# Row variance over 64 MB: increments of a semaphore at the end of two engines' programs, and a wait for them ahead of the clear

## The chip, the cores and the metric

The kernel runs on one core of one Trainium2 chip. The metric is the device time of one execution in microseconds (us). Three runs of the kernel before took 163.08, 163.54 and 163.08 us, a median of 163.08 us. The profiled execution took 163.1 us, and its span, from the first to the last of the program's own instructions, is 161.4 us.

## The reference: the variance of each row

The input is 32 x 512 rows of 1024 floats, 64 MB in all. For every row the kernel computes the mean of the squares less the square of the mean:

```python
mean_sq = np.mean(x**2, axis=-1)
sq_mean = np.mean(x, axis=-1)**2
return (mean_sq - sq_mean).astype(np.float32)
```

16,384 results are written, 64 KB.

## The kernel before

The 16,384 rows are laid on 128 partitions, 128 rows on each; the code calls one such row of every partition a column. `xt[0]` and `xt[1]` hold 16 columns each (8 MB a buffer). SyncE (SP in the profile) issues every load and every store, in the order in which they are written. Three turns of two buffers cover 96 columns; the last 32 columns come in pieces that grow smaller, `END_LOADS = [8, 8, 5, 4, 2, 2, 1, 1]`, and the very last column in two halves of 512 elements.

VectorE (DVE) and ScalarE (ACT) share the columns of each buffer. DVE takes a column with two BN_STATS of 512 elements and one BN_AGGR. ACT takes a column with two passes, `act_mean` (Copy with an accumulated sum, L122) and `act_var` (Square with the negative mean as bias and an accumulated sum, L127); the profile shows each of them as an ACTIVATE and an ACTIVATION_READ_ACCUMULATOR. In the loops ACT does 6 of 16 columns and DVE 10. In the last 32 columns the string `END_WHO` says who takes which; ACT has the column of the last full load, DVE the two halves after it. GpSimd (POOL) copies finished results and finishes 14 columns of the end from DVE's statistics.

Two details matter for the change. Both engines' programs are placed by `addr_align`, once, ahead of their loops (L145 and L146); in the profile that is a COMPARE_BRANCH of L146 on each of the two engines. The only code placed so is the engines' program from there on; nothing says where it ends.

The end of SP's program is a chain of waits and stores. The first store goes out after POOL's first copy (L304), the second when POOL, ACT and DVE have finished the columns before the last few (L306 to L309), and the third, 7 columns, when ACT has made its last step (L310, `act_step`) and DVE its last (L311, `dve_step`). SP then clears all semaphores but one (L313), waits for the three stores to land (L314) and clears the semaphore that they count (L315). The semaphores to clear are a range, from the first to the last in the list `sems` (L92).

DVE's program ends with the BN_AGGR of the last column (L262), which increments `dve_step`. ACT's program ends with the last `act_var` (L298), which increments `act_step`. After the program's own instructions the runtime's run: all engines meet, each resets a share of the semaphores, and they meet again.

Of the kernel before, what the change touches and what calls it, by code (L numbers as in the profile page):

```python
# [11 lines left out]
def kernel(  # L12
# [14 lines left out]
    nc = tc.nc  # L27
# [27 lines left out]
    PIECES = [512, 512]  # L55
    EARLY = 4
    HEAD = 128

    def sbuf(name, shape, dtype):
        return nc.alloc_sbuf_tensor(name, shape, dtype).ap()  # L60
# [19 lines left out]
    sync, act, dve, gps = nc.sync, nc.scalar, nc.vector, nc.gpsimd  # L80
    landed = [nc.alloc_semaphore(f"landed{b}") for b in range(NBUF)]
    NEND = len(END_LOADS) + len(PIECES)
    landed_end = [nc.alloc_semaphore(f"landed_end{b}") for b in range(NEND)]
    go = nc.alloc_semaphore("go")
    dve_done = nc.alloc_semaphore("dve_done")
    done = nc.alloc_semaphore("done")
    copied = nc.alloc_semaphore("copied")
    dve_step = nc.alloc_semaphore("dve_step")
    act_step = nc.alloc_semaphore("act_step")
    gps_step = nc.alloc_semaphore("gps_step")  # L90
    stored = nc.alloc_semaphore("stored")
    sems = [*landed, *landed_end, go, dve_done, done, copied, dve_step, act_step, gps_step]  # L92

    def load(dst, c0, n, sem, f0=0, f=D):
        b0, pitch, row0 = next(b for b in BLOCKS if b[0] <= c0 < b[0] + b[1])
# [7 lines left out]
    def store(c0, c1):  # L103
        b0, pitch, row0 = next(b for b in BLOCKS if b[0] <= c0 < b[0] + b[1])
        sync.dma_start(
            out=dataclasses.replace(
                out, offset=row0 + c0 - b0, ap=[[pitch, P], [1, c1 - c0]]
            ),
            in_=mv[:, 1, c0:c1],
        ).then_inc(stored, 16)  # L110
# [34 lines left out]
    for engine in (act, dve):  # L145
        engine.addr_align(FETCH_BLOCK_INSTRUCTIONS, offset=HEAD, max_nops=0)  # L146

# [113 lines left out]
    dve.wait_ge(dve_step, n)  # L261
    dve.bn_aggr(out=mv[:, :, c], in_=st).then_inc(dve_step, 1)  # L262
    dve_steps = n + 1

    act.preload_act_table(ACTF.Square)  # L265
    with nc.Fori(0, TURNS, engines=[ENG.Activation]):
# [18 lines left out]
    for b in range(len(END_LOADS)):  # L285
# [14 lines left out]
        last.then_inc(act_step, 1)  # L300
        act_step_of[b] = n
    act_steps = n

    sync.wait_ge(copied, 1)  # L304
    store(0, SMALL)
# [4 lines left out]
    sync.wait_ge(act_step, act_steps)  # L310
    sync.wait_ge(dve_step, dve_steps)  # L311
    store(early, ncols)
    sync.sem_clear(range(sems[0].num, sems[-1].num + 1))  # L313
    sync.wait_ge(stored, 48)  # L314
    sync.sem_clear(stored)  # L315
# [30 lines left out]
```

## Time and profile before

| | |
|---|---|
| median of three runs | 163.08 us |
| profiled execution, its own time | 163.1 us |
| its span | 161.4 us |
| DVE busy, ACT busy, POOL busy | 102.7, 106.9, 4.0 us |
| bytes read from HBM | 67.11 MB |
| load queue q1, share of 16 DMA engines' span | 97.1% |
| instruction queue q14 | 2 packets, 0.02 MB |

The times of single events below are microseconds from the span's start. A row of a group has the line in the kernel, the engine, the operation, what it writes from what it reads, the number of instructions, their busy time and the mean of one. SPq, ACTq and DVEq are the engines' sequencers: instructions that do no work on data, such as waits, increments and branches, are listed under these. Increments and waits that stand alone are EVENT_SEMAPHORE instructions, and clears of a range are EVENT_SEMAPHORE_RANGE_CLEAR. Besides instructions, the trace records each change of a semaphore and each packet of a DMA queue with its time; some times below are from these records.

### The profile page before, as it was taken

The numbers are of one execution on the slowest core, as the hardware profiler recorded it, in microseconds if no ns is written. First come the engines' busy times: TensorE is split into PE (matmuls) and PEld (weight loads), VectorE is DVE, ScalarE is ACT, GpSimd is POOL, SyncE is SP. The second block draws the span as 40 slices with busy tenths as digits, with TensorE's granted clock in tenths as the row PEclk, the third lists the DMA queues.
The fourth block names the chain that finished last, engine by engine and source line by source line (L and its number), as shares of the span: only waits on it lengthen the run. The fifth ranks groups of instructions, "written<-read, shape, count | busy, mean of one in ns | idle before, by whom it ended". The sixth has DMA issues, their size and how long they took to land. (4 is left out here: it accounts for less than half of the span.)

```text
span 161.4 us, 568 instructions
## 1 busy us (share of the span) xinstructions
DVE 102.7 (64%) x229; ACT 106.9 (66%) x189; POOL 4.0 (2%) x19
## 2 busy tenths in 40 slices
DVE  0000029980599607994099921999139999999894
ACT  3000039972599807996089941999339979999995
POOL 0000000000000000000000000000000000000700
DMA  7959969969969969969979979979969999899992
GB/s 264 520 260 520 520 276 503 520 276 503 520 276 503 520 276 504 520 292 487 520 309 471 520 325 455 520 325 455 520 276 471 422 406 479 380 424 416 426 396 77
DMA packets 2738, 67.19 MB, mean 416 GB/s; under 512 B 688, under 2 KB 688, under 8 KB 1200
## 3 DMA queue, kind: packets, MB, share of 16 engines
q1 hardware_dynamic: 2736, 67.18, 97.1%
q14 instruction: 2, 0.02, 0.1%
HBM read 67.11 MB, written 0.07 MB: 416 GB/s over the span
## 5 line engine op out<-in xcount | busy, mean ns | idle before, releaser
L118 DVE BATCH_NORM_STATS2 stats<-xt 128x6 f32<-128x512 f32 x120 | 71.8, 679 | 54.9 <-DVEq L114 54.9
L122 ACT ACTIVATE junk<-xt 128x1024 bf16<-128x1024 f32 x41 | 42.7, 1043 | 44.1 <-ACTq L114 43.7
L127 ACT ACTIVATE junk_sq<-xt,neg_mean 128x1024 f32<-128x1024 f32 x36 | 39.9, 1107 | 5.6 <-ACTq L114 4.1
L118 DVE BATCH_NORM_STATS2 stats_join<-xt 128x6 f32<-128x512 f32 x22 | 13.1, 681 | 0.0
L122 ACT ACTIVATION_READ_ACCUMULATOR junk<-xt 128x1 f32 x41 | 7.7, 187 | 0.0
L127 ACT ACTIVATE junk_sq<-xt_end,neg_mean_end 128x1024 f32<-128x1024 f32 x6 | 6.7, 1111 | 0.1
L127 ACT ACTIVATION_READ_ACCUMULATOR junk_sq<-xt,neg_mean 128x1 f32 x36 | 6.7, 187 | 0.0
L122 ACT ACTIVATE junk<-xt_end 128x1024 bf16<-128x1024 f32 x6 | 6.3, 1045 | 0.4 <-DMA xt_end<-in_x_dram 0.3
L220 DVE BATCH_NORM_AGGREGATE stage<-stats 128x2 f32<-128x12 f32 x60 | 5.1, 162 | 0.9
L127 ACT ACTIVATE junk_sq<-xt,neg_mean_end 128x1024 f32<-128x1024 f32 x5 | 5.5, 1105 | 0.1
L239 DVE BATCH_NORM_STATS2 stats_end<-xt_end 128x6 f32<-128x512 f32 x6 | 4.1, 683 | 0.6 <-DMA xt_end<-in_x_dram 0.6
L173 POOL COPY mv<-stage 128x32 f32<-128x32 f32 x3 | 0.6, 211 | 133.3 <-ACT junk_sq L127 133.3
L243 DVE BATCH_NORM_STATS2 stats_end<-xt_end 128x6 f32<-128x512 f32 x6 | 3.9, 646 | 0.0
L118 DVE BATCH_NORM_STATS2 stats_join<-xt_end 128x6 f32<-128x512 f32 x6 | 3.7, 692 | 0.0
L265 ACT ACT_TABLE_LOAD x1 | 1.3, 1283 | 2.8 <-PEq L153 2.8
L255 DVE BATCH_NORM_STATS2 stats_end<-xt_end 128x6 f32<-128x512 f32 x2 | 1.3, 668 | 0.6 <-DMA xt_end<-in_x_dram 0.6
L248 DVE BATCH_NORM_AGGREGATE mv<-stats_end 128x2 f32<-128x12 f32 x6 | 1.2, 194 | 0.0
L127 ACT ACTIVATION_READ_ACCUMULATOR junk_sq<-xt_end,neg_mean_end 128x1 f32 x6 | 1.1, 186 | 0.0
L122 ACT ACTIVATION_READ_ACCUMULATOR junk<-xt_end 128x1 f32 x6 | 1.1, 186 | 0.0
L127 ACT ACTIVATION_READ_ACCUMULATOR junk_sq<-xt,neg_mean_end 128x1 f32 x5 | 0.9, 186 | 0.0
L200 POOL TENSOR_SCALAR mv<-mu 128x6 f32<-128x6 f32 (+2 forms) x3 | 0.7, 238 | 0.3
L181 POOL TENSOR_TENSOR two<-stats_join 128x28 f32<-128x28 f32 x1 | 0.3, 273 | 15.0 <-DVE stats_join L118 15.0
(13 smaller groups left out, 2.8 us busy)
## 6 DMA issues: line engine op xcount, KB each, us to landing
xt<-in_x_dram SPq DMA_DIRECT2D x2, 4096.0 KB, 19.1
xt_end<-in_x_dram SPq DMA_DIRECT2D x1, 2560.0 KB, 29.4
xt_end<-in_x_dram SPq DMA_DIRECT2D x1, 2048.0 KB, 33.8
xt_end<-in_x_dram SPq DMA_DIRECT2D x2, 1024.0 KB, 36.8
xt_end<-in_x_dram SPq DMA_DIRECT2D x2, 512.0 KB, 38.9
xt_end<-in_x_dram SPq DMA_DIRECT2D x2, 256.0 KB, 39.6
xt<-in_x_dram SPq DMA_DIRECT2D x6, 24.1
out_dram<-mv SPq DMA_DIRECT2D x1, 52.5 KB, 4.4
```

The costliest lines, as they stand in the source:

```text
L118: last = dve.bn_stats(out=st[:, h, :], in_=xcol[:, h * H : (h + 1) * H])
L122: return act.activation(out=junk[i], in_=xcol, func=ACTF.Copy, scale=-S / D, accum_out=nm)
L127: return act.activation(out=junk_sq[i], in_=xcol, func=ACTF.Square, scale=S, bias=nm, accum_out=var)
L173: gps.tensor_copy(out=mv[:, 1, t * PER_TURN : (t + 1) * PER_TURN], in_=stage[:, :, 1]).then_inc(copied, 1)
L181: lambda: gps.tensor_tensor(out=two, in0=mean[:, :, 0:2], in1=mean[:, :, 2:4], op=ALU.add),
L200: lambda j=j, c=c, n=n: gps.tensor_scalar(out=mv[:, 1, c : c + n], in0=mu[:, j : j + n, 0], scalar1=1.0 / D, scalar2=None, op0=ALU.mult,)
L220: last = dve.bn_aggr(out=stage[:, j, :], in_=stats[:, j, :, :])
L239: dve.bn_stats(out=st[:, 0, :], in_=col[:, :H])
L243: dve.bn_stats(out=st[:, 1, :], in_=col[:, H:]).then_inc(dve_step, 1)
L248: return dve.bn_aggr(out=mv[:, :, c], in_=st)
L255: last = dve.bn_stats(out=st[:, i, :], in_=end_col(c)[:, f : f + size])
L265: act.preload_act_table(ACTF.Square)
```

## The change

A new semaphore `ended` is allocated and put into the list of those that SP clears. DVE increments it 8 times after its last BN_AGGR, ACT 16 times after its last `act_var`. These 24 increments are instructions of their own. SP waits until `ended` has reached 24 before its clear of the range. The wait stands behind the issue of the last store. Nothing else differs; the lines of the file move down by 3 to 8.

```diff
+    DVE_END = 8
+    ACT_END = 16
...
+    ended = nc.alloc_semaphore("ended")
     stored = nc.alloc_semaphore("stored")
-    sems = [*landed, *landed_end, go, dve_done, done, copied, dve_step, act_step, gps_step]
+    sems = [*landed, *landed_end, go, dve_done, done, copied, dve_step, act_step, gps_step, ended]
...
     dve.bn_aggr(out=mv[:, :, c], in_=st).then_inc(dve_step, 1)
     dve_steps = n + 1
+    for _ in range(DVE_END):
+        dve.sem_inc(ended, 1)
...
     act_steps = n
+    for _ in range(ACT_END):
+        act.sem_inc(ended, 1)
...
     store(early, ncols)
+    sync.wait_ge(ended, DVE_END + ACT_END)
     sync.sem_clear(range(sems[0].num, sems[-1].num + 1))
     sync.wait_ge(stored, 48)
     sync.sem_clear(stored)
```

## The prediction

> **What bounds the kernel now.** I read the page's head and its queues first, then the chain of waits that ended last, then the timeline of the last five microseconds, then SP's own waits. Page:
>
> ```profile
> span 161.4 us, 568 instructions
> ...
> DVE 102.7 (64%) x229; ACT 106.9 (66%) x189; POOL 4.0 (2%) x19
> ...
> q1 hardware_dynamic: 2736, 67.18, 97.1%
> q14 instruction: 2, 0.02, 0.1%
> ```
>
> The loads hold the 16 DMA engines for 97.1% of the span, and both compute engines are idle a third of it. The kernel is bound by its loads until they end. The second queue is the instructions': two packets in the whole span. The chain says the same, and what follows the loads:
>
> ```profile
> 118.15 39.35 DMA xt_end<-in_x_dram
> 157.50 0.02 issue
> 157.52 1.16 ACT junk L122 x2
> 158.68 0.02 issue
> 158.70 1.24 ACT junk_sq L127 x2
> ```
>
> The last full column lands at 157.50, and ACT's two passes over it, 1.16 and 1.24 us, end at 159.94. The change touches only what stands behind that. The timeline of the end:
>
> ```profile
> 158.91 0.64 DVE L255 BATCH_NORM_STATS2 stats_end<-xt_end 128x6 f32<-128x512 f32 x1
> 159.59 0.21 DVE L262 BATCH_NORM_AGGREGATE mv<-stats_end 128x2 f32<-128x12 f32 x1
> 159.75 0.19 ACT L127 ACTIVATION_READ_ACCUMULATOR junk_sq<-xt_end,neg_mean_end 128x1 f32 x1
> 159.97 0.33 SPq L105 DMA_DIRECT2D out_dram<-mv  x1
> ```
>
> The reader is to see that DVE ends at 159.80 and ACT at 159.94, that the last store is issued from 159.97 to 160.30, and that nothing computes after that. What is left of the span, 1.1 us, is SP's, and its waits name the one that ends last:
>
> ```profile
> SPq L311 <- DVE mv L262: 4.7, 1, 4.7
> SPq L315 <- DMA out_dram<-mv: 1.0, 1, 1.0
> ```
>
> By the records of single instructions the range clear (L313) runs from 160.343 to 160.407, and then SP sits until the store has landed at 161.361; the second clear runs from 161.378 to 161.403, the end of the span. So 0.97 us of SP's time after the first clear (161.378 less 160.407) is spent waiting for the store. That is the cover of the whole change.
>
> **The change part by part.**
>
> Sixteen increments on ACT. The nearest rows: in the loop a lone increment of `go` (L270) starts 72 ns after the wait before it (119.549 to 119.621, again 42.131 to 42.204 with 73), though the instruction itself lasts 17 ns. 16 x 72 = 1.15 us. When they start has two bounds. Late: they wait for ACT's last instruction and run from 159.94 to 161.09. Early: ACT's sequencer does not wait for its engine. In the loop's last turn the ALU_OP of L266 starts at 132.911, 39 ns after an ACTIVATE that runs to 133.989, and ahead of the read of the accumulator behind it; on DVE the ALU_OP of L211 starts at 132.164 while six of the ten BN_AGGR ahead of it have yet to start. A wait that is attached to an engine instruction does not seem to hold the sequencer either: `act_step` changes at 158.676 and the ACTIVATE that waits for it starts 23 ns later, where the standalone wait in the loop takes 94 ns (26.206 to 26.300). By these rows the increments run beside ACT's last passes and are done well before 159.94. I take early; late is kept as the bound.
>
> Eight increments on DVE. No row has a lone increment on DVE; a standalone wait lasts 21 ns there against 17 on ACT, and the next instruction of the sequencer comes 96 ns after one (2.680 to 2.776). 8 x 96 = 0.77 us at most, from 159.80 to 160.57 at the latest.
>
> What the sums mean for SP. It waits for 24 at the clear, which it reached at 160.343. Behind the waiting instruction on SP are only the clear, the wait for the stores and the last clear; the store is already issued, so nothing that moves data is held. Early: zero. Late: the clear starts at about 161.11 and ends at 161.18, still 0.20 us ahead of 161.378. Zero by both bounds. If the cover were gone, each further 0.1 us of the increments would be 0.1 us of the time.
>
> The clear takes one semaphore more. It clears 19 in 30 ns of records (160.356 to 160.386), so under 2 ns, in the same cover.
>
> The runtime's meeting. After ACT's end the records show three steps of the runtime's own semaphore at 160.053, 160.091 and 160.135, then nothing until 161.528, which follows SP's end at 161.403 by 125 ns. ACT may come about 1.3 us later without moving that. Late increments take 1.15 of it, so it holds: zero.
>
> Instructions fetched. DVE's program from the aligned place on is 120 instructions and ACT's 111 (counted in the trace: 252 and 233 executed from there, with two of the three turns of 66 and 61 taken off). They become 128 and 127. [...] The two q14 packets of the span are 8,192 bytes each, at 1.768 us (499 ns) and 1.932 us (956 ns), about 1.05 and 1.19 us after the two branches of L146 (0.718 ACT, 0.746 DVE). Before the span the same packets take 307 to 549 ns. Whether the longer programs call for another packet this profile cannot say. Bounds: zero, and 0.96 us if one such packet holds a DMA engine whose share of the last load ends last. I take zero, as the nearest row is the whole of the end of this program, where no q14 packet lies.
>
> [...]
>
> The sum: 163.1 us of the profiled execution (161.4 of span and 1.7 around it) + 0 + 0 + 0 = 163.1, which agrees with the median of 163.08.
>
> **The rivals.**
>
> *One more block of instructions (slower).* The two programs now end later in the instruction stream, and since the sequencers run ahead, the runtime's instructions behind them may be reached, and a further block called for, while the last loads are still in flight (until 158.56) or the last store is (packets at 160.79 to 160.98). For it: the two packets that followed the two branches, and their 499 and 956 ns beside loads against 307 alone. Against it: only two of 16 DMA engines would be hit, and the last half's increments come spread from 158.253 to 158.834, so an engine that is early by 0.3 us gives nothing away. One packet adds 0.31 to 0.96 us where it hits the last engine: 163.4 to 164.0. It decides the verdict where it costs over 0.49 us, 0.3% of the time, which is about what a measurement of this kernel can tell from no change.
>
> *Late and dear increments (slower).* If ACT's increments neither run ahead nor go at 72 ns, SP's clear passes 161.378 once each takes over 90 ns (1.44 us / 16). To be over the bound each has to take 120 ns or more: 163.6 and up. Against it: both rows of 72 and 73 ns.
>
> *The runtime's end gets shorter (faster).* After the last clear, 161.403, the runtime's semaphore steps at 161.528 to 161.690, resets end at 162.254, the second meeting runs from 162.479 to 162.835, and about 0.27 us after that has no record. If ACT and DVE come to the end of a loaded block inside that part, the longer programs would move that to where SP waits for the store. The price is the branch of L146: ACT's next instruction came 395 ns after it, DVE's 516, where SP's branch at 0.717 took 120 to the next, so 0.28 and 0.40 us more. One of these saved: 162.7 to 162.8; both in a row, 162.4. Against it: in the second meeting the steps are 34, 38, 44, 24, 97, 38, 35 and 46 ns, and the same meeting before the span has 34, 38, 43, 24, 112, 39, 34 and 46: no stall on ACT or DVE there, so only the last 0.27 us could hide one.
>
> *The change is not what it says.* If the increments were dropped, or joined into one each, nothing would move: that is 163.1 too, and counts with the forecast.
>
> **How the numbers follow.** Everything hidden, or nothing changed: 0.36, all within 0.3%. One more block: 0.30, of which 0.24 over the bound. Late increments: 0.04, all over it. A shorter end: 0.30, of which 0.24 beyond the bound (both savings) and 0.06 within; it gets that much because the last 0.27 us has no record that speaks against it, and a packet of instructions does matter after those two branches. So faster 0.24, same 0.36 + 0.06 + 0.06 = 0.48, slower 0.24 + 0.04 = 0.28. The time is that of the likeliest case, 163.1; its own range is 162.9 to 163.5, the scatter of the three runs. For 8 in 10 the range goes up to 164.0, the dearest single packet, and down to 162.4, both savings; beyond it lie increments far over 0.1 us each, two packets in a row, and an end shortened by more than the two branches' rows.
>
> **What the profile after would show.** 24 EVENT_SEMAPHORE rows more; ACT's starting before 159.9 (run ahead) or after it; their spacing near 72 ns. SP's wait for the stores still releasing the last clear, at about 161.38, and the span still 161.4 us. A third or fourth q14 packet would speak for the first rival, and its time against the last load's landing (157.50, 158.83) would give its cost. An unchanged span with a shorter time would speak for the third. The forecast is wrong if SP's last wait is no longer for the store, if the last loads land later, or if the 1.7 us around the span changes.

## The result, and the profile after

The changed kernel takes 163.86 us (median of 21 runs, 163.43 to 164.22) against 163.27 us (21 runs, 163.06 to 163.54). The ratio is 1.0032, with a 95% interval of 1.0026 to 1.0038: slower by 0.6 us. That is about the 0.3% which the prediction took as its bound, and the interval reaches to both sides of it. The profiled execution took 163.88 us, with a span of 162.565 us, so 1.31 us of its time are not in the span, where it was 1.70. Two things have moved, in opposite directions: the span is 1.16 us longer, and what is not in it is 0.38 us shorter. 1.16 - 0.38 = 0.78, and 163.1 + 0.78 is 163.88.

The page of the changed kernel:

```profile
span 162.6 us, 592 instructions
...
DVE 102.7 (63%) x229; ACT 106.9 (66%) x189; POOL 4.0 (2%) x19
...
q1 hardware_dynamic: 2736, 67.18, 96.4%
q14 instruction: 5, 0.03, 0.1%
```

The work of the engines and the load queue's packets are the same to the last digit. The instruction queue (q14) had two packets in the span; now it has five: by the records one of 24 bytes, the two of 8,192 bytes at 1.75 and 1.93 us as before, and two more of that size at 161.12 and 161.56 us. These two are new.

The timeline of the end, where all was expected to be hidden:

```profile
159.71 0.21 DVE L265 BATCH_NORM_AGGREGATE mv<-stats_end 128x2 f32<-128x12 f32 x1
159.88 0.19 ACT L130 ACTIVATION_READ_ACCUMULATOR junk_sq<-xt_end,neg_mean_end 128x1 f32 x1
160.09 0.33 SPq L108 DMA_DIRECT2D out_dram<-mv  x1
```

ACT ends at 160.07 and the last store is issued at 160.09, 0.13 us later than before, as the loads were in this execution. The increments themselves appear in the chain of waits as short pieces of ACT's sequencer, 72 ns apart, beside the last ACTIVATE:

```profile
159.65 0.06 issue
159.71 0.02 ACTq L309
159.73 0.06 issue
159.78 0.02 ACTq L309
159.80 0.06 issue
159.85 0.02 ACTq L309
159.87 0.01 issue
159.88 0.19 ACT junk_sq L130
```

They are done at 159.94, before ACT's engine is. DVE's are done at 160.40, and SP's clear runs from 160.477 to 160.543. The clear starts 50 ns after the store's issue ends, where it took 46 before, so the added wait holds SP for nothing. What holds it is the old wait, for the store. SP's waits (who waited for whom, us in total, times, longest), and the issue's time to landing, the last number of the row:

```profile
SPq L318 <- DVE mv L265: 4.7, 1, 4.7
SPq L323 <- DMA out_dram<-mv: 2.0, 1, 2.0
```

```profile
out_dram<-mv SPq DMA_DIRECT2D x1, 3.5 KB, 2.4
```

The same issue in the kernel before:

```profile
out_dram<-mv SPq DMA_DIRECT2D x1, 3.5 KB, 1.4
```

The 1.0 us of waiting has become 2.0, and a store that landed in 1.4 us now takes 2.4. The packet records say how. The store is 128 pieces of 28 bytes and 16 packets of 4 bytes, and `stored` steps 16 times for it: one part for each of the page's 16 DMA engines, as I read it. Fifteen parts land between 161.328 and 161.497. At 161.117 an instruction packet of 8,192 bytes starts and lasts 559 ns, to 161.676. At 161.672, as it ends, the last eight pieces of the store and their count go out, and this sixteenth part lands at 162.523, 1.03 us behind the fifteenth. The records do not name the DMA engine of a packet; that the instruction packet and the late part went through the same one is read from their order in time and from the counts, eight pieces of 128 and one part of 16. The second instruction packet (161.562, 531 ns) starts after the fifteen have landed.

### The profile page after: what moved, and what is told of

It is laid out like the page before. It is cut to its first block, busy times and chain, and to the rows that moved or that the text cites. A ratio compares the mean times of both kernels' runs of the same rounds, so it can differ in the third digit from the quotient of the medians.

```text
span 162.6 us, 592 instructions
## 1 busy us (share of the span) xinstructions
DVE 102.7 (63%) x229; ACT 106.9 (66%) x189; POOL 4.0 (2%) x19
```

## Theories and experiments

*Theory A, position.* The two packets at the start, 1.752 and 1.934 us, come 1.04 and 1.19 us behind the branches of L149 on ACT (0.717) and DVE (0.744). The theory takes the two new ones for the same: each of the longer programs comes to a place at which one more packet is called for (where the next "block" begins, in the words of the first rival and the expectations) while DMA traffic is still on the critical path. The packet follows about 1.1 us after the engine gets there, and the part of the store that meets it lands late. What ACT or DVE would have paid for the same packet in the runtime's part, outside the span, is saved there. No record shows what a packet holds or where a block ends; the records show when the packets come and what is late with them. *Theory B, the increments.* The 24 updates and the wait cost by themselves. *Theory C, chance.* The store's landing is late now and then, without relation to the packets.

The runs in one table. Packets are those of 8,192 bytes after the first two, in us from the span's start; "load end" is the start of the last load packet, "parts" the landing of the fifteenth and the sixteenth part of the last store, "around" the profiled time less its span. The ratios are against the kernel before, with 95% intervals; e1 to e4 ran on one chip and e5 to e8 on another, each beside the kernel before.

| kernel | extra packets | load end | parts | span | around | ratio |
|---|---|---|---|---|---|---|
| before | none | 158.56 | 161.33, 161.36 | 161.40 | 1.70 | 1 |
| changed | 161.12, 161.56 | 158.69 | 161.50, 162.52 | 162.57 | 1.31 | 1.0032 [1.0026, 1.0038] |
| e1, half | 162.69 | 158.49 | 161.24, 161.27 | 161.31 | 1.60 | 0.9992 [0.9984, 1.0001] |
| e2, DVE's alone | 161.59 | 158.71 | 161.49, 161.53 | 161.57 | 1.31 | 0.9970 [0.9957, 0.9982] |
| e3, ACT's alone | 161.15 | 158.65 | 161.42, 162.29 | 162.33 | 1.70 | 1.0048 [1.0036, 1.0060] |
| e4, both earlier | 152.43, 153.93 | 159.60 | 162.43, 162.46 | 162.50 | 1.32 | 1.0029 [1.0019, 1.0039] |
| e5, ACT's later | 161.54, 161.61 | 158.64 | 161.42, 161.43 | 161.49 | 1.32 | 0.9983 [0.9974, 0.9992] |
| e6, ahead of the loops | 155.22, 161.76 | 159.31 | 162.14, 162.90 | 162.94 | 1.32 | 1.0081 [1.0068, 1.0094] |
| e7, DVE earlier | 153.99 | 159.66 | 162.45, 162.47 | 162.51 | 1.32 | 1.0036 [1.0024, 1.0048] |
| e8, as e2 | 161.36 | 158.50 | 161.25, 161.28 | 161.32 | 1.31 | 0.9985 [0.9976, 0.9994] |

The table's events come from one execution of each kernel, but every run has its span on record, to 0.1 us. The 21 spans of the changed kernel are 162.1 to 162.9 us and the six of e3 are 162.1 to 162.4; the 47 of the kernel before, taken beside the experiments, are 161.3 to 162.0, and the 41 of e1, e2, e5 and e8 are 161.3 to 161.9. The part around the span is 1.66 to 1.75 us in every run of the kernel before and of e3, 1.46 to 1.70 in e1, and 1.26 to 1.36 in every run of the others. So the longer span and the shorter part around it belong to the kernels and not to single executions, which speaks against theory C.

### e1: half of the increments on each engine

```diff
-    DVE_END = 8
-    ACT_END = 16
+    DVE_END = 4
+    ACT_END = 8
```

> Half of the increments on each engine: 4 on VectorE, 8 on ScalarE, and SyncE waits for 12. Theory A (position in the instruction stream): after its last increment no engine has yet come to the place where the two extra instruction packets were called for, so no such packet lies before 161.4 us; the store lands 1.4 us after its issue, the span is 161.4 us, the time within 0.3% of the kernel before (162.8 to 163.4). Theory B (the increments and the wait themselves cost): about half of the loss, +0.25 to +0.35 us, and the store's landing or SyncE's clear is late in proportion. Theory C (the store's landing is late by chance): as likely late here as in the changed kernel, 163.9.

The kernel takes 163.06 us, a ratio of 0.9992 [0.9984, 1.0001]. SP's waits here:

```profile
SPq L323 <- DMA out_dram<-mv: 1.0, 1, 1.0
```

Twelve increments and the wait cost nothing that can be measured. Theory B, which wanted 0.25 to 0.35 us, falls. The one extra packet comes at 162.69, in the runtime's part, where nothing of the program is left to delay; the part around the span is 0.1 us shorter in this execution and varies from run to run, which stays unexplained.

### e2 and e8: VectorE's eight alone

```diff
-    ACT_END = 16
+    ACT_END = 0
```

> Only VectorE's 8 increments; SyncE waits for 8. Theory A: one extra packet, at about 161.5 us, called for about 1.1 us after VectorE's last increment at 160.4; the store's packets (160.8 to 161.1) are through by then, so the store lands at 161.4 and the span stays 161.4 us. If what the runtime does after the span (1.7 us before, 1.3 us with the change) is shortened by VectorE, the time is about 162.7; if by ScalarE, 163.1. Theory B: a third of the loss, +0.2 us, in SyncE's clear or the store. Theory C: 163.9 with a late store.

> VectorE's 8 increments alone once more, for the interval: 162.77 us and a ratio of 0.9970 the first time. By theory A the packet lies behind the store (161.6 us), the store lands 1.4 us after its issue, and the gain is the 0.38 us by which the runtime's part is shorter: ratio 0.997 to 0.998. If the first time was chance: 0.999 to 1.001.

The kernel takes 162.77 us, a ratio of 0.9970 [0.9957, 0.9982], and the second time 162.93 us, 0.9985 [0.9976, 0.9994]: faster than both kernels, twice, with intervals that meet at 0.998. The page of e2, and its issues:

```profile
span 161.6 us, 576 instructions
...
q14 instruction: 2, 0.02, 0.1%
```

```profile
out_dram<-mv SPq DMA_DIRECT2D x1, 3.5 KB, 1.4
```

The store lands in 1.4 us again. DVE's packet starts at 161.588, 0.02 us after the span's end, which is why the page still counts two; it comes 1.16 us after DVE's last increment (160.430), as in the changed kernel (1.17) and in e8 (1.16). And the part around the span is 1.31 us, as in the changed kernel. So the gain comes with VectorE's increments, and no loss with it.

### e3: ScalarE's sixteen alone

```diff
-    DVE_END = 8
+    DVE_END = 0
```

> Only ScalarE's 16 increments; SyncE waits for 16. Theory A: one extra packet, at about 161.1 us, 1.1 to 1.2 us after ScalarE's last increment; it is the one that held a DMA engine's share of the store in the changed kernel, so the store lands at about 162.4 in most executions and the span is 162.3 to 162.6 us; the time is 163.9 if VectorE shortens the runtime's part, 163.5 to 164.2 all told. Theory B: two thirds of the loss, +0.35 us, without a packet ahead of the store's. Theory C: as the changed kernel, with no relation to the packet.

The kernel takes 163.98 us, a ratio of 1.0048 [1.0036, 1.0060]. The issue of the last store, from e3:

```profile
out_dram<-mv SPq DMA_DIRECT2D x1, 3.5 KB, 2.3
```

One packet, at 161.148, 361 ns long. Fifteen parts of the store land by 161.421, the sixteenth at 162.290; its last pieces of 28 bytes go out at 161.5, as the packet ends. The part around the span is 1.70 us, as before. So the loss is ScalarE's. With e2 the changed kernel is the sum of the two: +0.0048 and -0.003 or -0.0015 make +0.0018 to +0.0033, against +0.0032.

### e5: ScalarE's increments, but the last one later

```diff
+    issued = nc.alloc_semaphore("issued")
...
-    for _ in range(ACT_END):
+    for _ in range(ACT_END - 1):
         act.sem_inc(ended, 1)
+    act.wait_ge(issued, 1)
+    act.sem_inc(ended, 1)
...
     store(early, ncols)
+    sync.sem_inc(issued, 1)
     sync.wait_ge(ended, DVE_END + ACT_END)
```

> The changed kernel with one order added: SyncE increments a further semaphore right after it has issued the last store, and ScalarE's sixteenth increment waits for it. ScalarE's program is as long as in the changed kernel, but its end is reached about 0.6 us later. Theory A (a packet of instructions meets the store): ScalarE's packet moves from 161.1 to about 161.7 us, behind the store's packets (over by 161.2), all 16 parts of the store land by 161.5, the span is 161.4 to 161.6 us and the time 162.7 to 162.9, as with VectorE's increments alone. Theory B (the 24 increments and the wait cost by themselves): as the changed kernel or worse, 163.9.

The kernel takes 162.89 us, a ratio of 0.9983 [0.9974, 0.9992]. It does everything that the changed one does, and more, and by the ratios it is 0.8 us faster. Its page counts as many packets as the kernel before, as both new ones lie behind the span's end at 161.485:

```profile
span 161.5 us, 593 instructions
...
q14 instruction: 2, 0.02, 0.0%
```

ACT's last increment is at 160.409 instead of 159.927; both packets come at 161.54 and 161.61, behind the store's pieces (over at 161.02), and all sixteen parts land by 161.43. Moving one packet by about half a microsecond takes the whole loss away. That decides between A and C: a store that is late by chance would not be late with the packet in e3 and the changed kernel, and in time without it in e2, e5 and e8.

### e6: the same increments ahead of the loops

```diff
+    for _ in range(DVE_END):
+        dve.sem_inc(ended, 1)
     with nc.Fori(0, TURNS, engines=[ENG.DVE]):
...
-    for _ in range(DVE_END):
-        dve.sem_inc(ended, 1)
...
+    for _ in range(ACT_END):
+        act.sem_inc(ended, 1)
     act.preload_act_table(ACTF.Square)
...
-    for _ in range(ACT_END):
-        act.sem_inc(ended, 1)
```

> The same 24 increments and the same wait, but ahead of the two engines' loops, where both wait 20 us for the first load; each program is as long as in the changed kernel, and its last instruction stands at the same place. Theory A: what costs is where and when a program comes to its next block. VectorE comes there about 0.65 us earlier than in the changed kernel, so its packet moves from 161.56 to about 160.9 us, right beside the store's packets; ScalarE's comes at 160.0 to 161.1. The store still lands late in most executions: span 162.0 to 162.6, time 163.3 to 164.0, and the runtime's part after the span is 1.3 us. Theory B: nothing is left at the end that could cost, so the kernel before: 163.1 to 163.3, span 161.4, 1.7 us after it.

The kernel takes 164.39 us, a ratio of 1.0081 [1.0068, 1.0094], the slowest of all, though none of the increments is at the end. ACT is late at its end again: its step into the runtime's meeting comes 442 ns after its last instruction's end, exactly as in the changed kernel, where it took 113 in the kernel before. Behind its packet (161.758) one part of the store lands at 162.900, 0.76 us after the fifteenth. VectorE's packet was expected at 160.9 and came at 155.2, among the loads, which then end 0.7 us late. The expectation had the cause but not the place of VectorE's packet, and time and span came out above its ranges (163.3 to 164.0 and 162.0 to 162.6 us).

### e4 and e7: programs moved, without increments

```diff
-    HEAD = 128
+    HEAD_ACT, HEAD_DVE = 147, 139
...
-    for engine in (act, dve):
-        engine.addr_align(FETCH_BLOCK_INSTRUCTIONS, offset=HEAD, max_nops=0)
+    for engine, head in ((act, HEAD_ACT), (dve, HEAD_DVE)):
+        engine.addr_align(FETCH_BLOCK_INSTRUCTIONS, offset=head, max_nops=0)
```

e7 is the same with `HEAD_ACT, HEAD_DVE = 128, 139`.

> The kernel before, no increments and no wait; instead the aligned place is moved by 19 instructions on ScalarE (offset 147) and by 11 on VectorE (139), so that by theory A the next block begins two or three instructions ahead of each engine's end: ScalarE comes there at about 157.6, VectorE at about 158.2, and both packets are called for when the loads have ended (158.7) and before the store's packets (160.8). Theory A: two extra packets at 158.6 to 159.9 us, the store lands at 161.4, the span is 161.4 us, the runtime's part after it is 1.3 us, the time 162.6 to 162.8, faster than both kernels. Theory B: no increments, so exactly the kernel before, 163.1 to 163.3, span 161.4. Theory C: 163.1 with a late store in some executions.

> The kernel before without increments, VectorE's program alone moved by 11 instructions (offset 139), ScalarE's left at 128. In e4 with both moved the packets came at 152.4 and 153.9 us, earlier than worked out, and the loads ended 0.9 us later. Theory A: one packet at 152 to 154 us, which costs the loads a share of that 0.9 us: last load 0.3 to 0.9 us late, the runtime's part 1.3 us, so the time is 163.0 to 163.6. If the late loads of e4 had nothing to do with the packets, the span is 161.4 and the time 162.7.

The kernels take 163.56 us, a ratio of 1.0029 [1.0019, 1.0039], and 163.80 us, 1.0036 [1.0024, 1.0048]. e4 was meant to put both packets into the gap between the loads and the store and to beat both kernels; it missed. The packets came some 6 us earlier than worked out, at 152 and 154 us, amid the loads. The chain of e7 shows what that does; the row is the last stretch of loads, which took 39.35 us in the kernel before:

```profile
118.30 40.30 DMA xt_end<-in_x_dram
```

A single packet of 8,192 bytes, 325 ns long, and the loads end 1.0 us later. The records of the loads' parts show that it is one part of sixteen again. The load that lands before the packet (153.99) has its last two parts at 152.49 and 152.60; of the next one the fifteenth lands at 155.04 and the sixteenth at 156.06, and this gap of 1.0 us stays to the last load (158.87 and 159.93). In the seven kernels without a packet among the loads they end between 158.49 and 158.71; in the three with one, at 159.31 to 159.66. Two packets (e4) cost no more than one: two parts are late there, the fifteenth by about 0.6 and the sixteenth by about 1.1 us behind the fourteenth, and the later one counts. The part around the span is 1.32 us in e4, e6 and e7, where VectorE's packet came at 153.93, 155.22 and 153.99 us: the saving came there too, so it did not need the packet near the end. But a packet among the loads cost more (0.7 to 1.05 us) than the saving gave (0.38).

## Why the prediction was right and wrong

**What bounds the kernel** was right: the loads, then ACT's last column, then the store. Nothing of it changed.

**Sixteen and eight increments: zero** was right in its result. 72 ns for ACT's spacing was right (72.5 measured), 96 for DVE's was a bound (92.7). The reading that they are "done well before 159.94" went too far; ACT's were done at 159.944. ACT's first increment starts at 158.834, 7 ns after the ACTIVATE ahead of it, which waits for `act_step`; DVE's first at 159.720, 14 ns after the BN_AGGR that waits for `dve_step`. Here the sequencer did not wait for its engine, but the attached wait of an instruction did hold it. The 23 ns had been read the wrong way. With this later start ScalarE's increments end when the loads are over (159.944 against 158.69), and its packet (161.117) falls beside the store.

**SP's wait and the runtime's meeting: zero** was right. SP's clear ended at 160.543, even ahead of the late bound of 161.18. ACT's step into the meeting slid from 160.05 to 160.51, within its 1.3 us.

**Instructions fetched: zero** is the step that failed. It should have been +1.03 us, the part of the store that came behind ScalarE's packet; the other 0.13 of the 1.16 us in the profiled pair is the scatter of the loads. I took zero because no instruction packet lay at the end of the program before; but the two packets that I had in hand, 1.05 and 1.19 us behind the branches of L146, were the nearer row. The rival *one more block* named the cause, the packets' duration (559 and 531 ns measured; 0.31 to 0.96 given) and the last store as a place. It priced a part's delay by the packet's length, and the delay is about twice that (1.03 us for 0.56 in the changed kernel, 0.87 for 0.36 in e3). By the prediction's own signs its mechanism was wrong: two more packets came, the span is 162.6 us, and the part around it is no longer 1.7 us.

**A shorter end**, the rival on the other side, was true as well. It gave 0.28 or 0.40 us for one engine; 0.38 was measured, and e2 and e3 show that it comes with VectorE alone. Most of its chance lay on both engines, and that did not happen. Its place was read wrongly. The prediction looked for it in the last 0.27 us, the profiled time less the last step of the runtime's second meeting. The same difference is -0.12 us in the changed kernel (163.88 less 164.001), so it is not a stretch of time behind the meeting. The records between do not hold the saving either: from the span's end to that last step it is 1.43 to 1.44 us in all ten profiled executions. The difference is -0.12 us in the seven where a packet of VectorE's came ahead of that meeting (e2, e4 to e8 and the changed kernel), 0.27 in the kernel before and in e3, and 0.17 in e1. That what is saved is a wait of VectorE for its packet of instructions fits the 0.40 us of the branch's row, but no record holds the saved time, so this last link is argued and not shown.

The forecast of 163.1 missed one term of +1.03 and one of -0.38; the small loss that came is what they leave. That the result lies within the forecast's 162.4 to 164.0, and within the first rival's 163.4 to 164.0, is in part luck: the delay alone is more than the 0.96 us of the dearest packet, and without the saving the profiled execution would have taken about 164.26 us, an estimate from 163.88 and 0.38. The narrow range of 162.9 to 163.5 was called the scatter of the three runs, which lie between 163.08 and 163.54.

In these runs the packets cost 0.76 to 1.03 us on the store (the changed kernel, e3, e6) and 0.7 to 1.05 on the loads (e4, e6, e7). They cost nothing in e2, e5 and e8, where the first came at 161.59, 161.54 and 161.36 us and the last part of the store had landed by 161.53, 161.43 and 161.28.

Open is why VectorE's packet came at 154 to 155 us when instructions were added ahead of its loop, or its place moved, and not near its end. By the count of instructions, with the 1.16 us that e2 and e8 show between VectorE's last increment and its packet, it was some 12 instructions early in e6 and e7, an estimate. ScalarE's packet was as early in e4 (152.43 us), while in e6 it came 1.04 us behind ACT's end, and in the changed kernel 1.05. Open is also why a late part of the store is later than its packet's length explains.

## What to carry to other kernels

In a kernel like this one, whose end is a chain of microseconds, the length of an engine's program can be a cost of its own: here its length and its place moved the instruction packets of 8,192 bytes between 152.43 and 162.69 us, and those that met the last loads or the last store cost 0.7 to 1.05 us. Look for such packets in the records of the instruction queue, and move them to where no transfer is waited for; here VectorE's eight increments alone do so, and the time falls by 0.15 to 0.3%. And when two engines get the same edit, run each alone: one gained 0.15 to 0.3% and the other lost 0.5%.

## What the hardware showed that I had not expected

- Where an 8,192-byte instruction packet (0.56 us long in the changed kernel, 0.36 in e3, 0.33 in e7) met a transfer, one part of its sixteen (two in e4) landed up to 1.0 us late: 1.03 us (changed), 0.87 (e3) and 0.76 (e6) on the store, and 0.7 to 1.05 us on the end of the loads (e4, e6, e7, against the mean of 158.6 of the kernels without). That packet and part share a DMA engine is read from their order in time. In the changed kernel the packet explains 0.56 of it; the part then also took 0.80 us from its last packet to its landing (0.74 in e3, 0.76 in e6), where the last part took 0.38 in the kernel before. Why it takes longer is open.
- Lone increments of the changed kernel are 72.5 ns apart on ScalarE and 92.7 on VectorE. ScalarE's ran beside its last pass (158.834 to 159.944, the pass 158.827 to 160.069). On neither engine did they start before the instruction ahead of them, which waits for a semaphore, had started (7 ns after it on ScalarE, 14 on VectorE).
